# Column sums for thirty-six norms: four 32-column strips of the array in place of two full-width products with ones

## The chip, the core and the metric

The kernel runs on one core of one Trainium2 chip. The metric is the device time of one execution in microseconds (us); the comparison is between the kernel before and the kernel after the change, each as a median of several runs.

## What is computed

The reference is one decoder layer on 2048 tokens of width 1024, in 32-bit floats. Cut to what matters here:

```python
def rms_norm(x, w):
    xf = x * lax.rsqrt(jnp.mean(x * x, axis=-1, keepdims=True) + EPS)
    return xf * w
def gated_head_norm(o, w, z):
    return o * lax.rsqrt(jnp.mean(o * o, axis=-1, keepdims=True) + EPS) * w * jax.nn.silu(z)
...
hn = rms_norm(h, pre_mix_norm); proj = hn @ w_in
o_a = gated_head_norm(gated_delta_rule(...), gdn_norm, z_gdn)    # 4 heads of 128
o_b = gated_head_norm(hgrn2(...), hgrn_norm, g_hg)               # 4 heads of 128
mix_out = concat(o_a, o_b) @ w_out
h = h + rms_norm(mix_out, post_mix_norm)
y = square(relu(rms_norm(h, pre_mlp_norm) @ w_mlp_up)) @ w_mlp_down
h = h + rms_norm(y, post_mlp_norm)
e = rms_norm(p @ w_ple_proj, ple_norm)
h = h + e * sigmoid(h @ w_ple_gate)
```

A norm needs, for every token, the sum of the squares of 128 (a head) or 1024 (an embedding) values. The kernel keeps features on the 128 partitions and tokens along the free dimension, so this sum runs across partitions.

## The kernel before, in words

The 2048 tokens are handled in four blocks of 512 (`q` from 0 to 3; `QT` is 512, `P` is 128, `NC` is 4, `SB` is 32). Nearly all matrix products are made with each operand split into two parts: a rounded part (type fp32r) and the rest. `split` (lines 170 to 173) makes the two parts: ScalarE copies the tile with rounding (L172), VectorE subtracts (L173). A product is then three TensorE matmuls of 128x128 by 128x512, high by high, high by low and low by high.

The work has four stages. First, the embeddings of the blocks 0 and 1 are projected (L199). Then comes the mixer stage: a list of input projections (L1134), three clock ticks each, with the head groups' work as Python generators that are advanced at ticks written out by hand (`A_STEPS`, `B_STEPS` and their like; `at(...)` puts them into an agenda, `tick()` and `half()` advance them). For each block there are four gated-delta heads (`gdn_mixer`) and four HGRN2 heads (`hgrn_mixer`); both end in `finish` (L602 to L619). Some of their small products are plain 32-bit float products of 128x128 by 128x128 (L681, L682, L753, L800, L884); the profile shows each of them as two matmuls with a weight load each, called two passes below. Third comes the output projection (L1017 and L1166), and fourth the MLP in a Strassen-like form and the gated embedding (L1166).

TensorE's and SyncE's instructions stand in program order where the schedule is marked manual; in the mixer stage and the MLP the order of ScalarE and VectorE is set by a scheduler.

The change is in `norm_steps` (L273 to L294), a generator that turns an accumulated tile of squares `acc` (128 partitions by 512 tokens) into the factor of each token. Before, it goes so:

- first step: `split` of `acc` into `hl` (L172 on ScalarE, L173 on VectorE)
- second step: two matmuls (L279 and L280) of `hl`'s two parts with a 128x128 tile of ones; all 128 rows of the result are the same 512 sums. ScalarE copies row 0 from PSUM into the first partition of `acc` (L282), and SyncE's queue stores this row to DRAM as `sd` (L284)
- third step: `sd` is loaded back as 128x4 (L287)
- then VectorE and GpSimd make the inverse root on 128x4 (L289, L168), it is stored as `rd` (L293), and later loaded broadcast to all partitions (L253)

`norm_steps` is run 36 times: 32 times from `finish` (4 blocks by 8 heads; tiles `nrm_g`, `hl_g`, `osq_g` for delta heads, `nrm_h`, `hl_h`, `osq_h` for HGRN2 heads), twice for the embeddings of blocks 0 and 1 near the start of the mixer stage and twice for those of blocks 2 and 3 late in the MLP (tiles `nrm_e`, `hl_e`, `acc_e`, in `late_embedding`). The norms of the model width (`rstd_steps`, L1191 and after: `nrm_o`, `nrm_y` and others) are another function with the same two matmuls at L1197 and L1198.

In `finish` the tile of squares is made by ScalarE (L606) and, for delta heads, a VectorE addition (L609).

Of the kernel before, what the change touches and what calls it, by code (L numbers as in the profile page):

```python
# [10 lines left out]
F32 = mybir.dt.float32  # L11
F32R = mybir.dt.float32r
BF16 = mybir.dt.bfloat16
U32 = mybir.dt.uint32
AF = mybir.ActivationFunctionType
# [5 lines left out]
P = 128  # L21
# [3 lines left out]
QT = 512  # L25
NQ = T // QT
NC = QT // P
# [4 lines left out]
SB = 32  # L32
# [64 lines left out]
def trunk(ctx, tc, x, xT, pT, vecs, w_in, w_ab, gdn_a_log, gdn_dt_bias, w_out, w_up, w_down,  # L97
          w_ple, w_gate, consts, out):
    nc = tc.nc
    V, S, G, PE = nc.vector, nc.scalar, nc.gpsimd, nc.tensor  # L100
# [5 lines left out]
    st = ctx.enter_context(tc.tile_pool(name="st", bufs=2))  # L106
# [3 lines left out]
    pp = ctx.enter_context(tc.tile_pool(name="pp", bufs=4, space=PSUM))  # L110
# [3 lines left out]
    def bank(name, pool=None):  # L114
        return (pool or pm).tile([P, QT], F32, tag="ps", name=name)

    def blk(c):
        return slice(c * P, (c + 1) * P)
# [43 lines left out]
    ones = cp.tile([P, P], F32R, name="ones")  # L162
# [4 lines left out]
    def rsqrt(v):  # L167
        G.tensor_tensor(v, v, mhalf, ALU.pow)  # L168

    def split(t, eng, raw):  # L170

        S.activation(t[:, 0], raw, AF.Copy)  # L172
        eng.tensor_tensor(t[:, 1], raw, t[:, 0], ALU.subtract)  # L173
# [56 lines left out]
    def squares(acc, src, k, name, eng=V):  # L230

        if acc is None:
            acc = st.tile([P, QT], F32, tag="acc", name=f"acc_{name}", bufs=3)
            S.activation(acc, src, AF.Square)
        else:
            turns[0] += 1
            if pair[0] and turns[0] % 2:
                sq = st.tile([P, QT], F32, tag="late", name=f"sq_{name}_{k}")
            else:
                sq = st.tile([P, QT], F32, tag="sq", name=f"sq_{name}_{k}", bufs=1)  # L240
            S.activation(sq, src, AF.Square)  # L241
            eng.tensor_tensor(acc, acc, sq, ALU.add)  # L242
        return acc
# [12 lines left out]
    def row_norm(acc, scale, eps, name):  # L256

        out = []
        for _ in norm_steps(acc, scale, eps, name, out.append):
            pass  # L260
        return out[0]
# [10 lines left out]

    def norm_steps(acc, scale, eps, name, done, pool=None):  # L273

        hl = st.tile([P, 2, QT], F32R, tag="hl", name=f"hl_{name}", bufs=1)
        split(hl, V, acc)
        yield
        ps = bank(f"nrm_{name}", pool or pp)
        PE.matmul(ps, ones, hl[:, 0, :], start=True, stop=False)  # L279
        PE.matmul(ps, ones, hl[:, 1, :], start=False, stop=True)  # L280
        row = acc[0:1, :]
        S.activation(row, ps[0:1, :], AF.Copy)  # L282
        sd = dr.tile([1, QT], F32, name=f"sd_{name}")
        nc.sync.dma_start(sd, row)  # L284
        yield
        m = sm.tile([P, NC], F32, tag="m", name=f"m_{name}")
        nc.sync.dma_start(m, sd.rearrange("o (p n) -> (o p) n", n=NC))  # L287
        yield
        V.tensor_scalar(m, m, scale, eps, ALU.mult, ALU.add)  # L289
        rsqrt(m)  # L290
        yield
        rd = dr.tile([1, QT], F32, name=f"rd_{name}")
        nc.sync.dma_start(rd.rearrange("o (p n) -> (o p) n", n=NC), m)  # L293
        done(rd)  # L294
# [162 lines left out]
    with mixers as mctx:  # L457
# [144 lines left out]
        def finish(q, h, pso, zt, extra, eps, n):  # L602

            og = st.tile([P, QT], F32, tag="late", name=f"og_{n}")
            sq = st.tile([P, QT], F32, tag="acc", name=f"osq_{n}", bufs=3)
            S.activation(sq, pso, AF.Square, scale=P ** -0.5)  # L606
            V.tensor_tensor(og, pso, zt, ALU.mult)
            if extra is not None:
                V.tensor_tensor(sq, sq, extra, ALU.add)  # L609
            rd = []  # L610
            yield from norm_steps(sq, 1.0, eps, n, rd.append)
            yield
            rsb = spread_load(rd[0], n)
            yield
            V.scalar_tensor_tensor(og, og, col(R_GNORM if h < 4 else R_HNORM), rsb, ALU.mult, ALU.mult)
            yield
            nc.sync.dma_start(mixd[q][h], og)
# [493 lines left out]
        for q in range(2):  # L1111
            at(0, norm_steps(accs[q], 1.0 / D, EPS, f"e{q}", partial(ple_r.__setitem__, q)),
               [4 * q + i for i in (0, 2, 4, 5, 6)])
        with tc.manual_schedule(engines={mybir.EngineType.SP}):
# [5 lines left out]
            for j, (name, key, src, q, h, then, g, b) in enumerate(works):  # L1120
# [3 lines left out]
                ps = bank(f"mm_{name}")  # L1124
# [288 lines left out]
    for j, (q, d) in enumerate(order):  # L1413
# [32 lines left out]
        if j in held:  # L1446
            ps = held.pop(j)
        elif order[j] == TOGETHER[0]:
# [5 lines left out]
            ps = held.pop(j)  # L1454
        else:
            ps = bank(f"mmo_{q}_{d}", pp)
# [3 lines left out]
        acc = square_sums[q] = squares(square_sums[q], ps, d, f"o{q}")  # L1460
# [403 lines left out]
    for half in range(2):  # L1864
# [4 lines left out]
        for d in range(KD):  # L1869
# [6 lines left out]
            for s, q in enumerate(qs):  # L1876
# [3 lines left out]
                ps = bank(f"mmg_{q}_{d}", pp)  # L1880
# [60 lines left out]
```

## Time and profile before

| | us |
|---|---|
| median of 3 runs | 2674.58 (2670.68 to 2675.51) |
| the profiled execution, time | 2671.73 |
| the profiled execution, span | 2669.9 |
| mean granted TensorE clock | 0.999 |
| TensorE busy (matmul) | 2639.4, 99% of the span |
| VectorE busy | 1963.1, 74% |
| ScalarE busy | 1491.8, 56% |

The profile is one execution, taken by the hardware profiler. Its time lies 1.8 us above its span, and 2.9 us under the median of the runs. Busy is the time in which at least one instruction of the engine (or of the group of a row) is under way; a matmul's end is modelled by the profiler, and the next one starts before it, so the start of one to the start of the next is the time that a matmul really takes from TensorE. PE is the matmuls, PEld their weight loads, DVE is VectorE, ACT ScalarE, POOL GpSimd and SP SyncE. L279 is line 279 of the kernel.

### The profile page before, as it was taken

The numbers are of one execution on the slowest core, as the hardware profiler recorded it, in microseconds if no ns is written. First come the engines' busy times: TensorE is split into PE (matmuls) and PEld (weight loads), VectorE is DVE, ScalarE is ACT, GpSimd is POOL, SyncE is SP. The second block draws the span as 40 slices with busy tenths as digits, with TensorE's granted clock in tenths as the row PEclk, the third lists the DMA queues.
The fourth block names the chain that finished last, engine by engine and source line by source line (L and its number), as shares of the span: only waits on it lengthen the run. The fifth ranks groups of instructions, "written<-read, shape, count | busy, mean of one in ns | idle before, by whom it ended". The sixth has DMA issues, their size and how long they took to land. (4 is left out here: it accounts for less than half of the span.)

```text
span 2669.9 us, 38295 instructions
## 1 busy us (share of the span) xinstructions
PE 2639.4 (99%) x12745; PEld 2210.5 (83%) x12745; DVE 1963.1 (74%) x4016; ACT 1491.8 (56%) x3025; POOL 136.4 (5%) x147
## 2 busy tenths in 40 slices
PE   8899999999999999999999999999999999999999
PEld 6788888888888888878888888888888888888887
DVE  7677767777677677578988867767877765468776
ACT  7776655466546556566556555555555555565422
POOL 0000000000000000010000000001000001101000
PEclk9999999999999999999999999999999999999999
DMA  8777777667666665683665576666544465687663
GB/s 279 278 239 248 246 252 248 230 230 252 218 208 224 226 218 187 197 248 107 222 219 198 175 243 218 208 208 214 197 170 144 164 230 190 195 254 251 207 220 131
DMA packets 267766, 573.51 MB, mean 215 GB/s; under 512 B 55578, under 2 KB 60152, under 8 KB 250416
## 3 DMA queue, kind: packets, MB, share of 16 engines
q1 hardware_dynamic: 265264, 566.86, 64.0%
q0 software_dynamic: 2304, 4.20, 0.9%
q8 instruction: 101, 1.65, 0.3%
q14 instruction: 97, 0.79, 0.1%
HBM read 410.57 MB, written 160.37 MB: 214 GB/s over the span
## 5 line engine op out<-in xcount | busy, mean ns | idle before, releaser
L1134 PE MATMUL mm<-xt,w 128*128 128x512 f32 x3072 | 783.8, 400 | 5.4 <-DVE acc_vg L564 3.1
L1134 PEld LDWEIGHTS mm<-xt,w 128*128 128x128 f32 x3072 | 553.1, 189 | 106.4 <-issue 3.7
L1166 PE MATMUL d<-db,da 128*128 128x512 f32 x2688 | 612.8, 389 | 0.0
L1166 PE MATMUL u<-t,wu 128*128 128x512 f32 x2604 | 591.8, 389 | 0.1
L1166 PEld LDWEIGHTS d<-db,da 128*128 128x128 f32 x2688 | 504.5, 188 | 104.8
L1166 PEld LDWEIGHTS u<-t,wu 128*128 128x128 f32 x2604 | 488.6, 188 | 102.3 <-ACT wu L172 0.5
L226 DVE TENSOR_TENSOR db<-db 128x512 fp32r<-128x512 f32 x224 | 159.5, 712 | 59.5 <-ACT db L225 59.1
L1564 DVE TENSOR_TENSOR u<-u,u 128x512 f32<-128x512 f32 x224 | 150.4, 682 | 53.5 <-PE u L1166 52.0
L225 ACT ACTIVATE db<-db 128x512 fp32r<-128x512 f32 x224 | 140.9, 629 | 63.9 <-DMA db<-hid 61.4
L1166 PE MATMUL mmg<-h2T,wg 128*128 128x512 f32 (+1 forms) x792 | 174.7, 383 | 0.0
L1166 PEld LDWEIGHTS mmg<-h2T,wg 128*128 128x128 f32 x792 | 145.5, 188 | 29.1
L1607 ACT ACTIVATE u<-u 128x512 f32<-128x512 f32 x128 | 80.7, 630 | 154.2 <-DVE u L1564 153.8
L173 DVE TENSOR_TENSOR da<-da 128x512 fp32r<-128x512 f32 x128 | 94.2, 736 | 92.1 <-ACT da L172 91.7
L172 ACT ACTIVATE da<-da 128x512 fp32r<-128x512 f32 x128 | 80.6, 630 | 128.1 <-DMA da<-sumd 109.0
L1166 PE MATMUL mmo<-mixT,w_out 128*128 128x512 f32 x600 | 137.9, 390 | 1.7 <-DVE w_out L173 1.0
L1166 PEld LDWEIGHTS mmo<-mixT,w_out 128*128 128x128 f32 x600 | 112.4, 188 | 26.2 <-DVE w_out L173 1.9
L172 ACT ACTIVATE wu<-a 128x512 fp32r<-128x512 f32 x124 | 75.1, 623 | 53.0 <-DMA a<-in_w_up_dram 50.7
L173 DVE TENSOR_TENSOR wu<-a,wu 128x512 fp32r<-128x512 f32 x124 | 86.0, 695 | 8.8 <-ACT wu L172 8.3
L173 DVE TENSOR_TENSOR da<-dr,da 128x512 fp32r<-128x512 f32 x96 | 68.3, 711 | 25.6 <-ACT da L172 24.4
L1608 ACT ACTIVATE u<-u 128x512 f32<-128x512 f32 x128 | 80.4, 628 | 3.0
L172 ACT ACTIVATE da<-dr 128x512 fp32r<-128x512 f32 x96 | 60.5, 630 | 34.0 <-DMA dr<-in_w_down_dram 26.8
L242 POOL TENSOR_TENSOR acc_y<-acc_y,sq_y 128x512 f32<-128x512 f32 x28 | 38.1, 1359 | 757.7 <-ACT sq_y L241 757.7
(393 smaller groups left out, 3838.9 us busy)
## 6 DMA issues: line engine op xcount, KB each, us to landing
w<-cache_in SPq DMA_DIRECT2D x96, 1024.0 KB
db<-hid SPq DMA_DIRECT2D x224, 256.0 KB
cache_in<-w SPq DMA_DIRECT2D x32, 1024.0 KB
hid<-u SPq DMA_DIRECT2D x128, 256.0 KB
da<-sumd SPq DMA_DIRECT2D x128, 256.0 KB
a<-in_w_up_dram SPq DMA_DIRECT2D x124, 256.0 KB
hid<-ht SPq DMA_DIRECT2D x96, 256.0 KB
dr<-in_w_down_dram SPq DMA_DIRECT2D x96, 256.0 KB
```

The source lines that it names most:

```text
L172: S.activation(t[:, 0], raw, AF.Copy)
L173: eng.tensor_tensor(t[:, 1], raw, t[:, 0], ALU.subtract)
L225: S.activation(t[:, 0], plain(t), AF.Copy)
L226: V.tensor_tensor(t[:, 1], plain(t), t[:, 0], ALU.subtract)
L242: eng.tensor_tensor(acc, acc, sq, ALU.add)
L1134: PE.matmul(ps, *terms[i], start=i == 0, stop=i == nt - 1)
L1166: PE.matmul(ps, a, b, start=start, stop=stop)
L1564: V.tensor_tensor(c[new], c[old], ps, ALU.add)
L1607: S.activation(c[k], c[k], AF.Relu)
L1608: S.activation(c[k], c[k], AF.Square)
```

## The change

`norm_steps` no longer splits `acc`. Its first step is now empty (the `yield` remains, so every later step keeps its tick). In the second step, in place of two matmuls of 512 tokens, there are four plain 32-bit float matmuls, one for each 128 tokens. Each uses 32 columns of the tile of ones as the weights and an own quarter of the array's columns (`tile_position=(0, c * SB)`), and writes 32 equal rows of 128 sums to the PSUM partitions 32c to 32c+31. ScalarE copies the whole 128x128 result into `acc`, and the store to `sd` takes the four partitions 0, 32, 64 and 96, 128 sums from each. The rest of the step, and `rstd_steps`, stay as they were.

```diff
     def norm_steps(acc, scale, eps, name, done, pool=None):
 
-        hl = st.tile([P, 2, QT], F32R, tag="hl", name=f"hl_{name}", bufs=1)
-        split(hl, V, acc)
         yield
-        ps = bank(f"nrm_{name}", pool or pp)
-        PE.matmul(ps, ones, hl[:, 0, :], start=True, stop=False)
-        PE.matmul(ps, ones, hl[:, 1, :], start=False, stop=True)
-        row = acc[0:1, :]
-        S.activation(row, ps[0:1, :], AF.Copy)
+        ps = bank(f"nrm_{name}", pool or pp)[:, :P]
+        for c in range(NC):
+            PE.matmul(ps[c * SB : (c + 1) * SB, :], ones.bitcast(F32)[:, :SB], acc[:, blk(c)], start=True, stop=True,
+                      tile_position=(0, c * SB))
+        S.activation(acc[:, :P], ps, AF.Copy)
         sd = dr.tile([1, QT], F32, name=f"sd_{name}")
-        nc.sync.dma_start(sd, row)
+        nc.sync.dma_start(sd.rearrange("o (c n) -> (o c) n", n=P), acc[::SB, :P])
         yield
```

## The prediction

> **What bounds the kernel now.** I read the page's busy times and the chain that ended last first, then busy time by stretches, then what TensorE waited for, then the rows of the norm itself.
>
> ```profile
> PE 2639.4 (99%) x12745; PEld 2210.5 (83%) x12745; DVE 1963.1 (74%) x4016; ACT 1491.8 (56%) x3025; POOL 136.4 (5%) x147
> ...
> PE 46%; DVE 1%; DMA 0%; issue 0%; ACT 0%; SPq 0%; DVEq 0%; ACTq 0%
> ```
>
> TensorE is at work for 99% of the span, and no other engine has a share of the chain that counts. Is its busy time real work, or is it stretched by waits? The stretches answer (columns: stretch, length, then busy us of PE, PEld, DVE, ACT and POOL with counts):
>
> ```profile
> 0.00:100.00 100.00, 83.82 (x350) 64.25 (x351) 70.68 (x154) 74.80 (x144) 7.22 (x22) 0.98 0.81 270
> 100.00:1060.00 960.00, 954.63 (x5271) 820.34 (x5271) 708.12 (x2021) 561.60 (x1452) 53.29 (x62) 1.00 0.71 234
> 1060.00:1200.00 140.00, 135.50 (x643) 112.33 (x642) 93.69 (x155) 85.13 (x148) 17.69 (x19) 1.00 0.74 220
> ...
> 1200.00:2000.00 800.00, 799.89 (x3528) 661.72 (x3527) 640.74 (x1006) 450.80 (x752) 19.48 (x14) 1.00 0.60 199
> ```
>
> From 1200 to 2000 us TensorE does nearly nothing but split products of 512 tokens: 799.9 / 3528 = 0.227 us each. That is the price of a 512-token matmul. In the mixer stage (100 to 1060 us), where 32 of the 36 norms lie, TensorE is without work for only 960 - 954.6 = 5.4 us; before 100 us, where two norms lie, for 16.2 us. So what the change does to TensorE's own time counts in full, and what it does for VectorE and ScalarE can win back a part of a few microseconds at most.
>
> **The change part by part.** The rows of what goes:
>
> ```profile
> L279 PE MATMUL nrm_g<-hl_g,ones x16: 389/395/494, 180.7 to 1104.9; 128*128 128x512 f32 x16
> ...
> L280 PE MATMUL nrm_g<-hl_g,ones x16: 388/393/502, 180.9 to 1105.1; 128*128 128x512 f32 x16
> L282 ACT ACTIVATE osq_g<-nrm_g x16: 586/587/588, 181.3 to 1105.5; 1x512 f32<-1x512 f32 x16
> ```
>
> ```profile
> 162.72 0.84 PE L1134 MATMUL mm<-xt,w 128*128 128x512 f32 x3
> 163.40 0.39 PE L279 MATMUL nrm_h<-hl_h,ones 128*128 128x512 f32 x1
> 163.62 0.39 PE L280 MATMUL nrm_h<-hl_h,ones 128*128 128x512 f32 x1
> 163.85 0.62 PE L1134 MATMUL mm<-xt,w 128*128 128x512 f32 x2
> ```
>
> *Removed from TensorE.* A row gives 0.39 us for one, but the starts are 163.40, 163.62 and 163.85: 0.225 us apart, in the middle of a full stream. I take 2 x 0.227 = 0.454 us for each norm, 36 x 0.454 = 16.3 us in all.
>
> *Added to TensorE.* Four plain float matmuls of 128 tokens. The trace has none with 32 columns or at a quarter of the array; the nearest are the 128-column ones:
>
> ```profile
> 505.09 0.39 PE L681 MATMUL kk_g<-y_kg 128*128 128x128 f32 x2
> 505.31 0.39 PE L682 MATMUL kk_g<-y_qg,y_kg 128*128 128x128 f32 x2
> 505.54 0.39 PE L681 MATMUL kk_g<-y_kg 128*128 128x128 f32 x2
> 505.76 0.39 PE L682 MATMUL kk_g<-y_qg,y_kg 128*128 128x128 f32 x2
> ```
>
> Each program matmul is two passes (x2), and one matmul starts 0.223 us after the other: 0.112 us a pass. So four matmuls are eight passes, and the whole question is how many of them run beside each other. Three bounds come from these rows:
> - one after another, as everything in this trace goes: 8 x 0.112 = 0.896 us
> - quarter by quarter in order, where the second pass of a quarter runs beside the first of the next: five slots, 5 x 0.112 = 0.56 us
> - all quarters at once: two passes, 0.224 us.
>
> The nearest row is the first; no row here shows two matmuls that share the array. I take 0.896 us: + 0.442 us for each norm, 36 x 0.442 = + 15.9 us.
>
> A second unknown is what it costs to go from the whole array to quarters and back. The nearest rows show TensorE starting again after a gap:
>
> ```profile
> 301.92 0.68 PE L753 MATMUL psp_g<-xn_g,um 128*128 128x128 f32 x4 [0.23 <-DMA xn_g<-xd_g]
> 302.46 0.71 PE L884 MATMUL at_h<-qk_h,keys_h 128*128 128x128 f32 x4
> 302.93 0.71 PE L1134 MATMUL mm<-xt,w 128*128 128x512 f32 x2
> ```
>
> ```profile
> L1134 PEld LDWEIGHTS mm<-xt,w 128*128 128x128 f32 x3072 | 553.1, 189 | 106.4 <-issue 3.7 <-ACT qk_h L829 1.7 <-ACT e_g L646 1.2
> ```
>
> Four passes after the gap take 0.54 us to the next group, where 4 x 0.112 = 0.448 us is the rule: 0.09 us for a start with nothing loaded ahead. The upper end is that the array runs empty (0.389 - 0.227 = 0.162 us from the rows of L279) and then loads weights uncovered (0.189 us, the mean of the last row), 0.35 us for a change. With two changes a norm, the ends are 0 and 36 x 0.70 = 25 us; by the row of the restart it is 36 x 0.18 = 6.5 us. In the forecast I take nothing, since these rows show gaps and not a change of shape; the price goes to a rival and the range.
>
> The Trainium skill speaks against the change here: "TensorEngine Tiling (Array Packing)", section Key Properties, says that changing the tiling mode, and not just the tile, drains TensorE. No row of this trace shows a change of mode; by that rule the 6.5 to 25 us would be added.
>
> *Removed from ScalarE and VectorE.*
>
> ```profile
> L172 ACT ACTIVATE hl_g<-osq_g x16: 617/632/635, 178.0 to 1102.4; 128x512 fp32r<-128x512 f32 x16
> L173 DVE TENSOR_TENSOR hl_g<-osq_g,hl_g x16: 668/684/693, 179.3 to 1103.7; 128x512 fp32r<-128x512 f32 x16
> ...
> L802 ACT ACTIVATE w_g<-psb_g,cc_g x64: 344/367/382, 142.2 to 1097.1; 128x128 f32<-128x128 f32 x64
> ```
>
> The split goes: 0.63 us of ScalarE and 0.68 us of VectorE a norm. The copy from PSUM is 128 elements long in place of 512, so nearer to the 0.367 us of L802 than to the 0.587 us of L282. Over 36 norms VectorE is spared 25 us and ScalarE 36 x 0.85 = 31 us. Both lie beside TensorE's work and cost nothing where they are, but a little of TensorE's waiting ends on them:
>
> ```profile
> PE mme L199 <- ACT pT L172: 9.5, 2, 7.3
> PE mm L1134 <- DVE acc_vg L564: 3.1, 1, 3.1
> PE nrm_o L1197 <- ACT hl_o L172: 2.6, 1, 2.6
> PE kk_g L681 <- ACT xt_g L776: 1.4, 1, 1.4
> PE mm L1134 <- ACT qk_h L829: 1.3, 1, 1.3
> ```
>
> The 9.5 us lie in the start, ahead of any changed norm, and the 2.6 us are another function. What can come back is the 3.1 us of `acc_vg` (at 75 us, with the two splits of the embeddings' norms ahead of it on VectorE: 1.4 us of it), and parts of the small ones. VectorE has 708 us of work in the 960 us of the mixer stage, so it isn't the bound there. I take -3 us, with 0 and -7 us as ends (5.4 us of idle time and 1.4 us before it). The scheduler also lets neighbours on VectorE and ScalarE trade places; that can go either way within these few microseconds.
>
> *Moved.* The four matmuls stand at the place of the two in TensorE's order, and the empty first step keeps every later step at its tick. TensorE now waits for the squares and not for the split, which took at least 1.3 us more (0.63 + 0.68): no wait is added, and nothing new is queued behind one. SyncE's and GpSimd's lists keep their order. The store `sd` takes four rows of 512 B in place of one of 2 KB; it and its load back end in a chain of loads and GpSimd's power, ticks away from the next use, so I cost it at nothing. If the cover were gone, VectorE's `og_g` would be late, and it waited for this chain already:
>
> ```profile
> DVE og_g L615 <- DMA rsb_g<-rd_g: 19.6, 12, 2.9
> ```
>
> That is VectorE's idle time, on an engine with a quarter of its time free.
>
> *Sum.* - 16.3 + 36 x 0.896 = 32.3, less 3: + 13 us. The profiled execution took 2671.73 us (span 2669.9 and 1.8 around it) and would take 2685. It lies 2.9 us under the median of the runs, 2674.58, against which the result is held: 2674.6 + 13 = 2688 us.
>
> **The rivals.**
>
> *1. All quarters at once.* 0.224 us for 0.454: 36 x -0.23 = -8.3 us, -3 with the waits: 2663 us, faster. For it: the four read other tokens and write other partitions, and nothing in the program orders them. Against it: no row shows such a thing, and the two passes of a quarter stand ahead of the next quarter's in the queue. "TensorE: Matmul & The Clock Gate" of the Trainium skill, Part 3, states this rule: matmuls at other tile positions run at the same time, starting about 4 ns apart. By it the time would be this one; this trace can't show it.
>
> *2. In order, with neighbours overlapped.* 0.56 us: 36 x 0.106 = + 3.8, - 3: + 1 us, 2676 us, no difference. Also here: one pass for each matmul in place of two, 4 x 0.112 = 0.448 us, so that the change doesn't bring the full 32-bit product its types say. With the price of two restarts, + 6.5, it is 2682 and belongs to the slower side.
>
> *3. The array runs empty at both changes of shape.* One after another, + 15.9 - 3, and 6.5 to 25 us on top: 2694 to 2713, about 2700. It decides from the first norm on, since 32 of 36 lie in full streams. For it: weights are loaded ahead of each matmul now (553 us of loads at L1134 lie beside the matmuls), which may not go on where the shape differs. Against it: going from 512-token split products to plain 128-token ones costs next to nothing here.
>
> *4. ScalarE and VectorE matter more.* All of the 7 us come back and the passes are as forecast: + 9 us, still slower, so it is inside the forecast's range.
>
> **How the numbers follow.** Forecast (eight passes one after another, or overlapped with a restart; 2680 to 2693): 0.40. Rival 1 (up to 2669): 0.16. Rival 2: 0.20. Rival 3: 0.24. About 0.2% (5.3 us) can be told from no change: faster is rival 1, 0.16; the same is rival 2 and the forecast's lower edge, 0.22; slower is the rest, 0.62. The range goes from rival 1's time to past the middle of rival 3: 2664 to 2705, leaving out about 0.08 below and 0.09 above. The forecast alone would be 2680 to 2693.
>
> **What would show it.** In the changed kernel's timeline, around a norm in a full stream (the one at 163 us, say): the time from the first pass of `nrm_h` to the next L1134 matmul's own pace, beside 0.45 us now. About 0.9 us with eight passes 0.11 us apart is the forecast; starts 0.03 us apart and about 0.25 us in all is rival 1; a gap of 0.2 us or more in front of the first or behind the last pass is rival 3. L282's successor should be near 0.37 us; busy time of VectorE should fall by some 25 us, ScalarE's by 31. I am wrong if the passes share the array, if each matmul shows one pass, or if idle time of TensorE in the mixer stage moves by more than 7 us.

## The result and the profile after

| | median us | ratio to before, 95% interval |
|---|---|---|
| before, 20 runs | 2672.27 (2667.45 to 2675.66) | |
| after, 20 runs | 2675.47 (2673.45 to 2680.36) | 1.0014 [1.0008, 1.0021] |

The change makes the kernel slower by about 3.7 us (0.14%; 2 to 6 us by the interval). That is clear of noise, but less than the 0.2% that the prediction called a difference, and much less than the 13 us that it forecast.

The page of the changed kernel first, the same two rows as before:

```profile
PE 2641.3 (99%) x12961; PEld 2201.9 (82%) x12961; DVE 1942.7 (73%) x3980; ACT 1459.0 (55%) x2987; POOL 137.8 (5%) x147
...
PE 87%; DMA 5%; DVE 3%; ACT 2%; issue 2%; POOL 0%; SPq 0%; DVEq 0%; POOLq 0%; ACTq 0%
```

TensorE has 216 matmuls more (288 passes in, 72 matmuls out). VectorE lost 20 us of busy time and ScalarE 33 us, where 25 and 31 were worked out. The shares of the chain can't be compared with those of before: it was followed back through nearly the whole span here, and through about half of it there. TensorE is most of it both times. Busy time by stretch (columns as before: PE, PEld, DVE, ACT, POOL):

```profile
0.00:100.00 100.00, 83.94 (x359) 64.03 (x360) 70.78 (x154) 71.83 (x141) 8.16 (x22) 0.97 0.83 277
100.00:1060.00 960.00, 953.17 (x5435) 811.14 (x5433) 689.68 (x1985) 533.63 (x1416) 52.73 (x61) 1.00 0.70 233
1060.00:1200.00 140.00, 135.73 (x665) 111.44 (x664) 91.53 (x154) 83.53 (x149) 18.87 (x20) 1.00 0.72 215
```

In the mixer stage VectorE has 18 us less to do and ScalarE 28, and TensorE's idle time is 960 - 953.2 = 6.8 us, where it was 5.4. So no idle time of TensorE came back there. Now the norm at 163 us, TensorE's matmuls in the changed kernel:

```profile
162.45 0.39 PE L1132 MATMUL mm<-xt,w 128*128 128x512 f32 x1
162.77 0.42 PE L278 MATMUL nrm_h<-osq_h,ones 128*32 128x128 f32 x8
163.13 0.73 PE L1132 MATMUL mm<-xt,w 128*128 128x512 f32 x2
```

Eight passes fill 0.42 us from the first start to the last end, and a single one lasts some 0.285 us (row below): eight in a row, 0.112 us apart, would fill 7 x 0.112 + 0.285, about 1.07 us. They share the array. To see what TensorE really gives for the norm, I count from the start of the last matmul ahead of it (162.45) to the start of the second one behind it (163.13 + 0.73 - 0.39 = 163.47), and take off the two matmuls that belong there: 1.02 - 2 x 0.227 = 0.56 us. The second one behind is used because the pause isn't over at the first: the two stand 163.47 - 163.13 = 0.34 us apart, where 0.227 is the pace. Counted so, the norm before cost 0.454 us. The difference of 0.10 us, 36 times, is 3.8 us, as large as the result.

That takes one norm for all 36. The traces of before and after, laid side by side from the second matmul ahead of each norm to the seventeenth behind it, say how far this holds. By this longer count the norm at 163 us costs 0.13 us more, and 0.13 us is also the median of the 20 norms of HGRN2 heads and embeddings. For the delta heads, most of which have smaller matmuls right behind them, the median is 0.04 us, from -0.13 to +0.13; the one at 306 us is left out of this, since TensorE waited 0.29 us there in the kernel before. The 35 others add up to +2.8 us, inside the measured 2 to 6. So the 3.8 us is right in size, but it isn't paid evenly.

```profile
L278 PE MATMUL nrm_h<-osq_h,ones x128: 272/285/297, 162.8 to 1092.5; 128*32 128x128 f32 x128
L280 ACT ACTIVATE osq_h<-nrm_h x16: 260/278/279, 163.3 to 1092.9; 128x128 f32<-128x128 f32 x16
```

Where the 0.56 us go is seen in the weight loads, changed kernel first and then the kernel before, around the same norm:

```profile
162.77 0.16 PEld L278 LDWEIGHTS nrm_h<-osq_h,ones 128*32 128x32 f32 x8 [0.35 <-ACT w_g L800]
163.12 0.76 PEld L1132 LDWEIGHTS mm<-xt,w 128*128 128x128 f32 x4 [0.20 <-issue]
```

```profile
163.18 0.19 PEld L279 LDWEIGHTS nrm_h<-hl_h,ones 128*128 128x128 f32 x1
163.40 0.19 PEld L280 LDWEIGHTS nrm_h<-hl_h,ones 128*128 128x128 f32 x1
163.63 0.64 PEld L1134 LDWEIGHTS mm<-xt,w 128*128 128x128 f32 x3
```

Before, the load for a matmul starts about 0.22 us ahead of it (163.18 for the matmul at 163.40), beside the matmul then under way. After, the first load for the strips starts with the first strip pass (162.77), and the first load behind the strips starts with its matmul (163.12 and 163.13): nothing is loaded ahead across either border. The brackets show the weight port without work for 0.35 and 0.20 us. (The first bracket names a ScalarE copy as the last thing to come; but the same 0.32 us from the matmul ahead to the first strip pass stand in every strip kernel below, none of them shows TensorE's matmul waiting, and in the run on the whole array, whose matmuls need the same squares, it is 0.23 us. So I put it down to the border.)

### The profile page after: what moved, and what is told of

Read it like the earlier page. It is cut to its first block, busy times and chain, and to the rows that moved or that the text cites. A ratio compares the mean times of both kernels' runs of the same rounds, so it can differ in the third digit from the quotient of the medians.

```text
span 2672.9 us, 38659 instructions
## 1 busy us (share of the span) xinstructions
PE 2641.3 (99%) x12961; PEld 2201.9 (82%) x12961; DVE 1942.7 (73%) x3980; ACT 1459.0 (55%) x2987; POOL 137.8 (5%) x147
## 4 chain that ended last, share of the span: by engine, by line
PE 87%; DMA 5%; DVE 3%; ACT 2%; issue 2%; POOL 0%; SPq 0%; DVEq 0%; POOLq 0%; ACTq 0%
PE u L1164 23%; PE d L1164 23%; PE mm L1132 21%; PE mmg L1164 7%; PE mmo L1164 3%; PE mmo L1015 1%; PE at_h L882 1%; PE mm_ab L1132 1%; PE mme L199 1%; DMA mixT<-mixd 1%; DMA xs<-in_x_dram 1%; PE pso_h L918 1%; PE pso_h L919 1%; PE psa_g L793 0%; PE psc_g L803 0%
```

## The experiments

Theory A, formed from these rows: all four strips run at once, two passes of 0.112 us for the whole norm, and each norm pays some 0.33 us on top for going from the whole array to strips and back. Rival B: the strips run in order with neighbours overlapped, five slots of 0.112 us, 0.56 us too, and the border is free. Rival C: the spared work of ScalarE and VectorE gives time back, and the strips' price is larger than it looks. The cost of a norm in the table is counted as above, at the one norm near 163 us, from the rows shown below (for the split kept and rounded twice, from the same rows of their traces); "worked out" is 36 times its difference from 0.454 (32 times for rounded squares).

| run | cost of a norm, us | worked out, us | median | ratio to before, 95% interval | in us |
|---|---|---|---|---|---|
| after | 0.56 | +4 | 2675.47 | 1.0014 [1.0008, 1.0021] | +2 to +6 |
| split kept as well | 0.56 | +4 | 2679.12 | 1.0022 [1.0012, 1.0032] | +3 to +9 |
| strips twice | 0.79 | +12 | 2687.85 | 1.0055 [1.0041, 1.0069] | +11 to +18 |
| all on one strip | 1.20 | +27 | 2699.38 | 1.0094 [1.0080, 1.0108] | +21 to +29 |
| two strips of 64 | 0.79 | +12 | 2686.04 | 1.0047 [1.0033, 1.0061] | +9 to +16 |
| whole array, plain float | 0.91 | +16 | 2690.43 | 1.0065 [1.0053, 1.0078] | +14 to +21 |
| rounded, summed twice | 0.454 | 0 | 2674.56 | 1.0004 [0.9995, 1.0013] | -1 to +3 |
| rounded, summed once | 0.227 | -7 | 2669.23 | 0.9981 [0.9972, 0.9990] | -7 to -3 |

Each ratio is against runs of before made beside it (medians 2672.39 for the split kept, strips twice, one strip and rounded twice, 2673.59 for the others).

**Strips twice.** This tells A from B: what does a second set cost, when the border is paid already?

```diff
-        for c in range(NC):
+        for c in (*range(NC), *range(NC)):
             PE.matmul(ps[c * SB : (c + 1) * SB, :], ..., tile_position=(0, c * SB))
```

> The changed kernel with the four strip matmuls issued twice in a row in each norm (the second four write the same sums again). Theory A (two passes of 0.112 us for all four strips at once, plus 0.33 us once for entering and leaving): 0.224 us more for each norm, +8 us over the changed kernel, +11 against before. Rival B (the strips don't really run at once; 0.556 us is five slots of 0.112 us in order, with no price for the change of shape): 8 slots of 0.112 more or less, some 0.45 us more for each norm, +16 us over the changed kernel, +19 against before.

TensorE's matmuls around the norm:

```profile
164.97 0.39 PE L1132 MATMUL mm<-xt,w 128*128 128x512 f32 x1
165.28 0.64 PE L278 MATMUL nrm_h<-osq_h,ones 128*32 128x128 f32 x16
165.86 0.74 PE L1132 MATMUL mm<-xt,w 128*128 128x512 f32 x2
```

165.86 + 0.74 - 0.39 - 164.97 - 0.454 = 0.79 us: eight passes more cost 0.22 us more, which is two slots and not four. The time, +11 to +18 us, holds A's +11 at its edge and leaves out B's +19 only narrowly. B falls on the trace.

**All on one strip.** The border stays, the sharing goes.

```diff
-        ps = bank(f"nrm_{name}", pool or pp)[:, :P]
+        ps = bank(f"nrm_{name}", pool or pp)
...
-            PE.matmul(ps[c * SB : (c + 1) * SB, :], ones.bitcast(F32)[:, :SB], acc[:, blk(c)], start=True, stop=True,
-                      tile_position=(0, c * SB))
-        S.activation(acc[:, :P], ps, AF.Copy)
+            PE.matmul(ps[:SB, blk(c)], ones.bitcast(F32)[:, :SB], acc[:, blk(c)], start=True, stop=True,
+                      tile_position=(0, 0))
+        row = acc[0:1, :]
+        S.activation(row, ps[0:1, :], AF.Copy)
...
-        nc.sync.dma_start(sd.rearrange("o (c n) -> (o c) n", n=P), acc[::SB, :P])
+        nc.sync.dma_start(sd, row)
```

> The changed kernel with all four matmuls on the first strip of 32 columns, each writing its own 128 columns of the same 32 rows; ScalarE copies one row of 512 as before the change. Theory A: eight passes one after another, 0.896 us, plus 0.33 us for the change of shape: 1.23 us for each norm, +24 us over the changed kernel, +28 against before. Rival B (no price for the change of shape): 0.9 us for each norm, +12 us over the changed kernel, +16 against before.

```profile
163.28 0.39 PE L1133 MATMUL mm<-xt,w 128*128 128x512 f32 x1
163.60 1.06 PE L278 MATMUL nrm_h<-osq_h,ones 128*32 128x128 f32 x8
164.59 0.73 PE L1133 MATMUL mm<-xt,w 128*128 128x512 f32 x2
```

The same eight passes now fill 1.06 us, and the norm costs 164.59 + 0.73 - 0.39 - 163.28 - 0.454 = 1.20 us: eight slots, 0.896, and 0.30 for the border.

**Whole array, plain float.** The passes without a border: just the price that the prediction took.

```diff
...
-            PE.matmul(ps[c * SB : (c + 1) * SB, :], ones.bitcast(F32)[:, :SB], acc[:, blk(c)], start=True, stop=True,
-                      tile_position=(0, c * SB))
-        S.activation(acc[:, :P], ps, AF.Copy)
+            PE.matmul(ps[:, blk(c)], ones.bitcast(F32), acc[:, blk(c)], start=True, stop=True)
+        row = acc[0:1, :]
+        S.activation(row, ps[0:1, :], AF.Copy)
...
```

> The changed kernel with the four plain float matmuls on all 128 columns of the whole array, one for each 128 tokens; ScalarE copies row 0 of 512 as before the change. No change of shape. This is the price that the prediction took: eight passes of 0.112 us one after another, 0.896 us a norm in place of 0.454: +16 us against before, +12.5 over the changed kernel. By the rival that plain float passes in a row are cheaper among split products: under +10.

Matmuls, and then weight loads:

```profile
164.61 0.39 PE L1132 MATMUL mm<-xt,w 128*128 128x512 f32 x1
164.84 1.05 PE L278 MATMUL nrm_h<-osq_h,ones 128*128 128x128 f32 x8
165.65 0.71 PE L1132 MATMUL mm<-xt,w 128*128 128x512 f32 x2
```

```profile
164.62 1.08 PEld L278 LDWEIGHTS nrm_h<-osq_h,ones 128*128 128x128 f32 x8
165.62 0.53 PEld L1132 LDWEIGHTS mm<-xt,w 128*128 128x128 f32 x3
```

The first pass starts 0.23 us after the matmul ahead of it, as in a full stream (0.32 us in every kernel with strips), and its weights are loaded from 164.62 on, ahead of it. 165.65 + 0.71 - 0.39 - 164.61 - 0.454 = 0.91 us, +16 us worked out, +14 to +21 measured, which leaves out the under +10 of the rival. Against "all on one strip", which has the same passes one after another, the strip costs 0.29 us more: that is the border, in two kernels whose matmuls differ in the strip and its 32 columns of ones alone. Which of the two makes the border, no run tells.

**Two strips of 64 columns**, 256 tokens each.

```diff
...
-        for c in range(NC):
-            PE.matmul(ps[c * SB : (c + 1) * SB, :], ones.bitcast(F32)[:, :SB], acc[:, blk(c)], start=True, stop=True,
-                      tile_position=(0, c * SB))
+        for c in range(2):
+            PE.matmul(ps[c * 64 : (c + 1) * 64, :], ones.bitcast(F32)[:, :64], acc[:, c * 2 * P : (c + 1) * 2 * P],
+                      start=True, stop=True, tile_position=(0, c * 64))
...
```

> The changed kernel with two strips of 64 columns and 256 tokens each in place of four of 32 and 128. Theory A (strips at once, plus 0.33 us for entering and leaving): two passes of 0.215 us, 0.76 us a norm, +11 us against before, +7.5 over the changed kernel. Rival B (in order with neighbours overlapped, no price for the change): three slots of 0.215 us, 0.645 us, +7 against before, +3.5 over the changed kernel.

```profile
162.47 0.39 PE L1132 MATMUL mm<-xt,w 128*128 128x512 f32 x1
162.79 0.65 PE L278 MATMUL nrm_h<-osq_h,ones 128*64 128x256 f32 x4
163.37 0.73 PE L1132 MATMUL mm<-xt,w 128*128 128x512 f32 x2
```

0.79 us again: two slots of 256 tokens, 0.43 (the two passes of L866 in the kernel before, 128x256, start at 366.38 us and the matmul behind them at 366.81), and 0.35 for the border. The measured +9 to +16 us holds A's +11 and leaves out B's +7.

**Strips of different width.** One look, for the order of the passes.

```diff
-            PE.matmul(ps[c * SB : (c + 1) * SB, :], ones.bitcast(F32)[:, :SB], ...
+            m = SB - 8 * c
+            PE.matmul(ps[c * SB : c * SB + m, :], ones.bitcast(F32)[:, :m], ...
...
```

> One look: the changed kernel with 32, 24, 16 and 8 columns of ones in the four strips, so that the rows of the trace tell the strips apart; ScalarE copies the four result rows one by one. Theory A: the first pass of all four strips starts before the second of any, about 0.007 us apart, and the second passes 0.11 us later. Rival B: both passes of a strip stand together, and the next strip follows.

The strip matmuls that start up to 163.84 us, with the forms and their counts at the end of the row; the first starts at 163.8:

```profile
L279 PE MATMUL nrm_h<-osq_h,ones x4: 277/289/297, 163.8 to 163.8; 128*32 128x128 f32 x1, 128*24 128x128 f32 x1, 128*16 128x128 f32 x1, 128*8 128x128 f32 x1
```

One pass of each of the four strips has begun before the second pass of any. (This kernel ran once, in 2681.76 us, with four short copies in place of one; its time isn't compared.) So the two passes of one matmul aren't held together; the run says nothing of whether they are issued in this order or overtake each other.

**The split kept as well**, with nothing that reads it: TensorE's part of the change alone.

```diff
     def norm_steps(acc, scale, eps, name, done, pool=None):
 
+        hl = st.tile([P, 2, QT], F32R, tag="hl", name=f"hl_{name}", bufs=1)
+        split(hl, V, acc)
         yield
```

> The changed kernel, with the split of the squares kept on ScalarE and VectorE although nothing reads it: TensorE's part of the change alone. Theory A (TensorE alone: a norm takes 0.556 us of it in place of 0.454, because the array is emptied and reloaded at each change of shape; ScalarE and VectorE give nothing back): 36 x 0.10 = +3.7 us against before, so within 1.5 us of the changed kernel. Rival C (relief hides a part: the spared splits give TensorE 3 us or more back, and the price of the strips is larger than it looks): 3 to 7 us slower than the changed kernel, +6 to +10 against before.

+3 to +9 us, where the changed kernel has +2 to +6. By the ratios it is 2.1 us slower than the changed kernel, more than A's 1.5 and less than C's 3; the intervals overlap, and the run can't tell A from a small C. (In this kernel's profiled execution the granted clock is 0.50 from 308 to 316 us, after TensorE waited 1.64 and 1.33 us, so its own span isn't used.) The next run is the better test.

**Rounded squares, summed twice.** The relief of ScalarE and VectorE alone, at TensorE's old work: the squares of the 32 head norms are written rounded, both matmuls take them, and the sum is halved. The low part of the squares is left out; the four norms of the embeddings keep their split.

```diff
-        hl = st.tile([P, 2, QT], F32R, tag="hl", name=f"hl_{name}", bufs=1)
-        split(hl, V, acc)
+        if acc.dtype == F32R:
+            parts = (acc,) * 2
+        else:
+            ...
-        PE.matmul(ps, ones, hl[:, 0, :], start=True, stop=False)
-        PE.matmul(ps, ones, hl[:, 1, :], start=False, stop=True)
+        for i, part in enumerate(parts):
+            PE.matmul(ps, ones, part, start=i == 0, stop=i == len(parts) - 1)
...
-            sq = st.tile([P, QT], F32, tag="acc", name=f"osq_{n}", bufs=3)
+            sq = st.tile([P, QT], F32R, tag="acc", name=f"osq_{n}", bufs=3)
...
```

> The kernel before, with the split gone for the 32 head norms: their squares are written rounded to fp32r, and both full-width matmuls take them (the sum is halved on the way out), so the low part of the squares is left out. TensorE's work is that of before; ScalarE loses 32 x 0.63 us and VectorE 32 x 0.68 us. Theory A: relief is worth nothing, within 1.5 us of before. Rival C: 3 to 7 us faster than before.

1.0004 [0.9995, 1.0013], -1 to +3 us: C's 3 to 7 us are out. Relief of the two engines in the head norms is worth at most about 1 us here.

**Rounded squares, summed once.** The same with `parts = (acc,)`: no split, one matmul of 512 tokens, no border. The low part is left out again.

> The kernel before with the squares of the 32 head norms written rounded to fp32r and summed by one full-width matmul in place of two; the split of these squares is gone, and their low part is left out. No change of shape and half of the work: 32 x 0.227 = 7.3 us less of TensorE's time; theory A (TensorE's time counts in full, relief nothing): -7 us against before, 2665. With relief (rival C): -10 to -14.

```profile
162.76 0.62 PE L1141 MATMUL mm<-xt,w 128*128 128x512 f32 x2
163.21 0.39 PE L284 MATMUL nrm_h<-osq_h,ones 128*128 128x512 f32 x1
163.44 0.39 PE L1141 MATMUL mm<-xt,w 128*128 128x512 f32 x1
```

0.9981 [0.9972, 0.9990], 3 to 7 us faster than before, with the forecast 7 at the edge. The runs pointed on to a version that takes one full-width matmul from every norm:

**The high part alone in all 48 norms** (`norm_steps` and `rstd_steps`).

```diff
-        split(hl, V, acc)
+        S.activation(hl[:, 0], acc, AF.Copy)
         yield
         ps = bank(f"nrm_{name}", pool or pp)
-        PE.matmul(ps, ones, hl[:, 0, :], start=True, stop=False)
-        PE.matmul(ps, ones, hl[:, 1, :], start=False, stop=True)
+        PE.matmul(ps, ones, hl[:, 0, :], start=True, stop=True)
```

> The kernel before with the high part of the squares alone in all 48 norms (36 of heads and embeddings, 12 of the model width): ScalarE's rounding copy stays, VectorE's subtraction and the second full-width matmul go, so the low part of the squares is left out. Theory A (TensorE's time counts in full): 48 x 0.227 = 10.9 us faster than before, 2662; a fall in VectorE's busy time of some 33 us adds nothing. Rival C (relief of VectorE counts too): 14 to 18 us faster. If TensorE's time counted only in part, 3 to 7 us.

2663.37 us against 2673.52 of before on its chip, 0.9965 [0.9952, 0.9979]: 6 to 13 us faster, with the forecast of 10.9 inside. It beats both kernels, at the price of the squares' low part.

## Why the prediction was wrong, point by point

- **What bounds the kernel**: right. TensorE's time counted in full: over the nine timed kernels the worked-out sums run from -11 to +27 us, and every one lies within its interval. (Three of the 32 head norms, at 1068, 1090 and 1105 us, stand behind the stretch from 100 to 1060 us that the prediction put all of them in; nothing in its sum rests on that.)
- **Removed from TensorE**, 0.454 us a norm: right, and shown by the runs with one matmul less (0.227).
- **Added to TensorE**, "I take 0.896 us": this is the step that failed. Eight passes one after another are the price of the whole array or of a single strip (0.91 and 1.20 us with the border, both measured). On four strips they take two slots, 0.224 us, the lowest of the three bounds: -8.3 us over 36 norms, where + 15.9 was put down. It was argued that the nearest row was the serial one; but every row of the trace was serial because no kernel line used a strip, so these rows couldn't speak on it.
- **The price of the change of shape**, taken as nothing, "the price goes to a rival": also wrong, and of the other sign: 0.33 us, some + 12 us over 36 norms, which hid half of the first error of 24 us. With - 8.3, + 12 and nothing from the other engines the sum comes to 3.7. The border is 0.30 to 0.35 us a norm in four kernels (after, twice, one strip, two strips), between the restart's 0.18 and the upper 0.70; by the longer count it is some 0.03 us more in a full stream. Rival 3 named what is seen there: weights aren't loaded ahead across the border. The Trainium skill says in "TensorEngine Tiling (Array Packing)", Key Properties, that a change of mode drains TensorE; the pause of 0.33 us for in and out in this trace is in line with that. Whether the array must be empty or the missing load alone makes the pause isn't told apart by these runs.

 The prediction also says that the trace of before has no row for a change of shape. It has some, which were overlooked: L541's transposes use 36 rows of the array and stand in a full stream. TensorE's matmuls and then the weight loads, in the kernel before:

```profile
59.39 0.39 PE L1134 MATMUL mm<-xt,w 128*128 128x512 f32 x1
59.71 0.25 PE L541 MATMUL ps_gb<-cst,gb 36*128 36x36 f32 x1
59.80 0.23 PE L541 MATMUL ps_gb<-cst,gbb 36*128 36x36 f32 x1
59.86 0.23 PE L541 MATMUL ps_gb<-cst,gb 36*128 36x36 f32 x1
59.92 0.23 PE L541 MATMUL ps_gb<-cst,gbb 36*128 36x36 f32 x1
60.08 0.73 PE L1134 MATMUL mm<-xt,w 128*128 128x512 f32 x2
```

```profile
59.71 0.13 PEld L541 LDWEIGHTS ps_gb<-cst,gb 36*128 36x128 f32 x1 [0.35 <-issue]
60.07 0.30 PEld L1134 LDWEIGHTS mm<-xt,w 128*128 128x128 f32 x2
```

 The marks are those of the strips: 0.32 us from the matmul ahead to the first pass, 0.34 us between the two behind, the weight port without work for 0.35 us, no load ahead on either side. Counted as above, 60.08 + 0.73 - 0.39 - 59.39 - 0.454 = 0.58 us, of which four passes some 0.06 us apart are about 0.25: about 0.33 us are left for the border. So a price for it could be read before the change, and 36 x 0.33 = 12 us by this row would have been the term. With the passes still one after another that would have moved the forecast further off, to 2700 us: the sharing is the step on which the sum failed.
- **Rival 1** had the passes right, but priced no border: -8.3 us of TensorE where +3.7 came. The Trainium skill's rule in "TensorE: Matmul & The Clock Gate", Part 3, is that matmuls at other tile positions run at the same time, their starts about 4 ns apart; this trace agrees on the first, and has the first passes of the four strips some 7 ns apart (at 163 us they start 318, 325, 331 and 338 ns behind the matmul ahead of them). **Rival 2** gave 2676, close to the 2675.5 measured, but by luck, with a mechanism that isn't there: its 0.56 us are five slots, the real 0.56 are two slots and a border. "Strips twice" is what parts them.
- **ScalarE and VectorE**, "I take -3 us": wrong, nothing came back that the runs can tell from none. The wait of 3.1 us at 75 us on `acc_vg` is the plain case. After the change it reads so:

```profile
75.21 1.22 PE L1132 MATMUL mm<-xt,w 128*128 128x512 f32 x2 [3.30 <-ACT zt_zg L597]
```

```profile
72.63 0.61 ACT L672 ACTIVATE q_g<-y_qg 128x512 f32<-128x512 f32 x1
73.26 1.28 ACT L597 ACT_TABLE_LOAD   x1
74.56 0.60 ACT L597 ACTIVATE zt_zg<-mm 128x512 f32<-128x512 f32 x1
```

 VectorE is no longer last there, but ScalarE's `zt_zg`, behind a table load of 1.28 us, is late at the same place, and TensorE waits 3.3 us.
- **Moved**: right as far as seen. The store in four rows and the shorter copy (0.278 us, where 0.367 was taken) made no new wait of TensorE.

## What to carry to other kernels

A small matmul put on strips of the array must be priced in two parts: the passes, which do share the array, and the border into and out of the strips, paid once for each visit whatever is done in it (0.3 us here, more than a full-width matmul of 512 tokens). In a stream of full-width matmuls, strips are worth while for many passes in one visit, not for one norm at a time. An estimate from "strips twice": two norms in one visit would take 0.79 us, where two norms before take 0.91; no run has tried it. And where a trace has no row for a mechanism, as here for the sharing, the nearest row is no estimate of it. For the border it had one, on a line that had nothing to do with the norms: search the whole trace by the shape of the matmuls before calling a price unknown. Both unknowns were bounded rightly and then set at the wrong ends.

## What the runs showed of the hardware that was not expected

- The four strips take plain float operands at full pace together: 0.22 us for eight passes of 128 tokens (twice against once), and two strips of 64 columns do the same with 256 tokens.
- The first passes of all four matmuls start ahead of every second pass: by 163.84 us in the run with strips of different width, 0.04 us after the first of them, and no second pass has begun by then.
- A copy from PSUM of 128 partitions by 128 took 0.278 us on ScalarE, of one partition by 128 0.269 (in the run with strips of different width), and of one by 512 0.587: the time went with the length of a row here, and 128 times the rows cost 0.01 us.
- A visit of 36 rows of the array paid a border of the same size as one of 32 or 64 columns: about 0.33 us at 59.7 us in the kernel before. Where such a visit stands right behind a norm (near 559 and 812 us), the strips cost 0.13 and 0.11 us less than the two full-width matmuls by the longer count: a part of the border was paid there already.
